# Encoder layer on one core: a fourth z unit, tile-wise waits and re-ordered block sums in the gate section; a one-operation T1, later evictions and later T4 lows in gate/up

## The chip, the cores and the metric

The kernel runs on one core of a Trainium2 chip. The metric is the device time in microseconds (us) of one execution; a kernel's time is the median of its runs. Five engines work from queues of their own, each strictly in its program's order, and meet only through semaphores: TensorE (PE, matrix products into PSUM banks), VectorE (DVE), ScalarE (ACT), GpSimd (POOL) and SyncE (SP), which here issues the DMAs.

## The reference, cut to what matters

One layer of a hybrid encoder on 1024 tokens and 16 meta tokens with 1024 columns, all in float32:

```
h    = rmsnorm(x);  proj = h @ w_in     # q|k|v|z|beta,a|B|C|x|gate_a|gate_b
o_dn = bidirectional gated DeltaNet(q, k, v, beta, a), normed, times silu(z)
y_a  = o_dn @ w_branch_dn
y_b  = (B * conv3(C * x)) @ w_branch_sc
x    = x + (sigmoid(gate_a) * y_a + sigmoid(gate_b) * y_b) @ w_out
gu   = rmsnorm(x) @ w_gate_up
x    = x + (silu(gu[:, :2816]) * gu[:, 2816:]) @ w_down
out  = rmsnorm(x) * final_norm_w
```

## The kernel before, in words

Every float32 operand is split into a high and a low part (`split`: ACT casts the high part, DVE subtracts to get the low one), and a product is three matmuls: high by high, high by low, low by high. So each operand of PE costs one ACT and one DVE operation before PE can read its second half.

**Phase 1** (to 946 us) runs the DeltaNet heads. Its order is written by a planner in the code (`pick`, `run_streams`, `pump`) under a manual schedule: the dense products of `w_in` (a *unit* is 128 columns: 8 blocks of k by 3 matmuls for each half of the tokens) fill PE between the steps of the scans. `ZH` of the eight z units are among these fillers; in the kernel before, five.

**The gate section** (946 to about 1089 us) computes the other z units (`z_rows`) and five gate pairs (`pair`, for columns `j` = 3 to 7 of `gate_a` and `gate_b`). A pair is computed in Strassen's way with seven block products instead of eight: the four blocks B11, B12, B21, B22 of the activations (2 halves of k by 2 halves of the tokens) give the sums T1 to T4 once (`moving_sums`, a generator whose steps the code interleaves with the z units), and the weights give S1 to S4 for each pair (`sums`, `stationary2`). The seven products, 12 matmuls each (`product`), are A11·B11, A12·B21, S2·T2, S1·T1, S3·T3, S4·B22 and A22·T4. They add up in two PSUM banks, `bank` and `bank2`, which are read ("evicted") between products: a partial sum that is read must be read before the next product adds to the same bank.

The z units, the sums and the first pair stand inside `border0`, a manual schedule for DVE, PE and ACT, so on these engines they keep the order in which the code writes them; a scheduler may put later work between them, and orders the rest. All tiles of this section come from the pool `tp`, which takes over the memory of phase 1's pools. Weights pass through four `raw` slots, loaded by SP.

**Branch, merge and output products** follow (to 1344 us), then **gate/up** (`part1` for A11·B11 and A12·B21, and the loop over `j` for the other five products, again with T1 to T4, for 22 column units), whose first units lie under a manual DVE schedule (`border`). There the moving blocks are built 128 tokens at a time by `norm_T` and `second_half`: T1 = B12 - B11, T2 = B22 - T1, T3 = B22 - B12, and T4 = B21 - T2 in `form_T4`. At the end stands the down product.

Of the kernel before, what the change touches and what calls it, by code (L numbers as in the profile page):

```python
# [16 lines left out]
P = 128  # L17
D = 1024
KT = 8
# [6 lines left out]
NC = 8  # L26
FF = 2816
NF = FF // P
ZH = 5
GH = 3  # L30
EPS = 1e-6
NEG = -1e30
# [16 lines left out]
def encoder_layer(ctx: ExitStack, tc: tile.TileContext, x, meta, norm1_w, w_in, w_ba,  # L49
# [128 lines left out]
    def sub(out, a, b):  # L178
        nc.vector.tensor_tensor(out=out, in0=a, in1=b, op=ALU.subtract)
# [6 lines left out]
    def norm_T(t, diag, hn, bank=psany):  # L186

        c = slice(t % 4 * P, t % 4 * P + P)
        pts = []
        for g in range(2):  # L190
            pt = bank().rearrange("p (k t) -> p k t", k=4)
            pts.append(pt)
            for k in range(4):
                kk = 4 * g + k
                piece = hn[:, kk * P:(kk + 1) * P]
                if diag is None:
                    transpose(pt[:, k], piece)
                else:
                    mm(pt[:, k], piece, diag, start=True, stop=True)
            if t < 4:  # L200
                split(*(m[:, :, c] for m in mov[("B11", "B21")[g]]), pt)
        if t < 4:
            return

        def blocks():
            second_half(c, pts)
        return blocks

    def second_half(c, pts):
        b11h, b11l = (m[:, :, c].bitcast(F32) for m in mov["B11"])  # L210
# [1202 lines left out]

    def sums(rg, ru, s2, s4_, s3, s1):
        g0, g1, u0, u1 = rg[:, 0:4], rg[:, 4:8], ru[:, 0:4], ru[:, 4:8]
        nc.vector.tensor_tensor(out=s1, in0=u0, in1=u1, op=ALU.add)
        sub(s3, g0, u0)
        sub(s2, s1, g0)
        sub(s4_, g1, s2)

    def stationary2(j, ru, sa, sb, A_):

# [8 lines left out]
        split(uh, ul, ru[:, 4:8])  # L1431
        A_["A22"] = uh, ul

    def product(po, a, b, add_to=False):

        (ah, al), (bh, bl) = a, mov[b]
        for k in range(4):
            bhk, blk = (m[k] if isinstance(m, list) else m[:, k] for m in (bh, bl))
            for x, y, i in ((ah, bhk, 0), (ah, blk, 1), (al, bhk, 2)):
                mm(po, x[:, k], y, start=k + i == 0 and not add_to, stop=k == 3 and i == 2, skip_group_check=add_to)  # L1440

    def moving_sums():

# [52 lines left out]
    def z_rows(h):  # L1496

        sz = s4(SEQ)
        for sl in (left, right):
            po = psany()  # L1500
            dense(po, z_units[h - ZH], hx, C0 + META + sl.start, 512)
            nc.scalar.activation(sz[:, sl], po, AF.Tanh, scale=0.5)
            yield
            nc.vector.scalar_tensor_tensor(out=sz[:, sl], in0=sz[:, sl], scalar=1.0, in1=po, op0=ALU.add, op1=ALU.mult)
        nc.sync.dma_start(z_d[h], sz)
        yield
# [3 lines left out]
    def pair_weights(n, j):  # L1510

        s_hl[n % 2] = big(("mB", "mA")[n % 2], [P, 2, 2, KT, P])
        if n == 0:
            u = big("w2", [P, 2, 4, P])
            u_hl[0] = u[:, 0], u[:, 1]
        elif n == 1:
            u_hl[1] = [tp.tile([P, 4, P], F32R, tag="t2", name=uid("u_hl"), bufs=2) for _ in range(2)]
        gh, gl = wtiles([P, KT, P])
        rg, ru = (rawtile([P, KT, P]) for _ in range(2))
        nc.sync.dma_start(rg, w_in[unit(OGA + j * P)])  # L1520
        nc.sync.dma_start(ru, w_in[unit(OGB + j * P)])
# [10 lines left out]
        return A_, first, second  # L1532

    def pair(n, j, A_, first, second):

        last = j == KT - 1
        o1, o2 = s4(), s4()
        bank = pss()
        if not last:
            if n:  # L1540
                first()
            product(bank, A_["A11"], "B11")
            nc.scalar.copy(o1[:, left], bank)  # L1543
            po = psz()
            product(po, A_["A12"], "B21")
            add(o1[:, left], po, o1[:, left])
            half_turn(o1[:, left])
        if last:
            first()
        if n:  # L1550
            second()
        bank2 = psz()
        if not last:
            product(bank, A_["S2"], "T2", True)
            nc.scalar.copy(o1[:, right], bank)
            product(bank2, A_["S1"], "T1")
            nc.scalar.copy(o2[:, right], bank2)
            product(bank, A_["S3"], "T3", True)
            add(o2[:, right], bank, o2[:, right])
            half_turn(o2[:, right])  # L1560
            product(bank2, A_["S4"], "B22", True)
            add(o1[:, right], bank2, o1[:, right])
            half_turn(o1[:, right])
            product(bank, A_["A22"], "T4", True)
            nc.scalar.activation(o2[:, left], bank, AF.Tanh, scale=0.5)
        else:
# [19 lines left out]
            half_turn(o1[:, right])  # L1586
        nc.sync.dma_start(ta_d[j], o1)
        nc.sync.dma_start(tb_d[j], o2)
        return o1
# [8 lines left out]
    z_units.append(wload(w_in, unit(OZ + (H - 1) * P)))  # L1598
    next(sums_of_blocks)
    next(z0)  # L1600
    next(z1)
    pair0 = pair_weights(0, GH)
    next(z1)
    pair0[1]()
    next(z1)
    pair0[2]()
    next(z2)
    next(sums_of_blocks)
    next(z2)
    next(sums_of_blocks)  # L1610
    next(sums_of_blocks)
    next(z2)
    next(sums_of_blocks)
    for n, j in enumerate(range(GH, KT)):
        o1 = pair(n, j, *(pair_weights(n, j) if n else pair0))
        if n == 0:
            border0.close()
# [115 lines left out]
    def part1(w, p1, sg):  # L1733
# [7 lines left out]
        add(sg, po, p1)  # L1741
        nc.scalar.activation(sg, sg, AF.Silu)
        return rg, ru, A_, p1, sg, bank

    def down_sums(k):

# [47 lines left out]
    for i in range(2):  # L1794
        split(t1s[i], t1s[2 + i], m32[1][:, 2 * i:2 * i + 2])
    p1_2 = [tp.tile([P, 512], F32, tag="t2", name=uid("t2"), bufs=2) for _ in range(2)]
    ahead.append(part1(w2, *p1_2))
    split(*mov["T3"], m32[3])
    u_hl[0] = big("w2", [P, 2, 4, P])
    for j in range(NF):  # L1800
        if j == 1:
            s_hl[1] = ap_.tile([P, 2, 2, KT, P], F32R, tag="al0", name="s_hl1")
            u_hl[1] = ap_.tile([P, 2, 4, P], F32R, tag="al2", name="u_hl1")
        rg, ru, A_, p1, sg, bank = ahead.pop(0) if ahead else part1(stationary1(j), sm[:, j % 2], sm[:, 2 + j % 2])
        if j:
            block22(j, ru, A_)
            sums(rg, ru, rg[:, 0:4], rg[:, 4:8], ru[:, 0:4], ru[:, 4:8])
# [25 lines left out]
        product(bank, A_["A22"], "T4", True)  # L1833
        mul(sg, bank, sg)
        if j == 0:
            border.close()
# [151 lines left out]
```

## Time and profile before

| | before |
|---|---|
| runs | 2009.29, 2007.11, 2007.06 us; median 2007.11 |
| the profiled execution | 2003.46 us, of it the span 2001.7 us |
| granted TensorE clock | 0.996 |
| PE busy | 1974.2 us (99%), 11999 matmuls |
| DVE / ACT / POOL busy | 1398.8 / 837.2 / 108.0 us |
| DMA | 251.00 MB, mean 125 GB/s |

PE is busy for 99% of the span, and the chain that ended last runs through it. A busy PE in this profile is not PE at its peak: a matmul's record lasts 0.39 us, while the next one starts 0.227 us after it, and records overlap. So lost time on PE is read from the starts of matmuls, not from its busy share: it hides in the short stretches where starts are further apart, or where the granted clock is low.

### The profile page before, as it was taken

The page shows a single profiled execution, that of the slowest core. Times are in us where ns is not written, and L with a number is a line of the kernel's source. Part 1 is how long each engine was busy: PE and PEld are TensorE (multiplying, and loading weights), DVE is VectorE, ACT ScalarE, POOL GpSimd, SP SyncE. Part 2 cuts the span into 40 slices and gives each one's busy share as a digit, 9 for nine tenths or more (in the row PEclk, how much of TensorE's full clock was granted, in tenths as well). Part 3 has the DMA queues.
Part 4 walks back from the last instruction along what each step waited for, and adds up shares of the span by engine and source line. Part 5 has one row for each costly group of instructions (what it writes and reads, how often), then busy time and mean ns, then how long its engine had stood idle before and what let it go on. Part 6 is the DMA issues. An engine that isn't in the chain of part 4 may idle for free.

```text
span 2001.7 us, 31862 instructions
## 1 busy us (share of the span) xinstructions
PE 1974.2 (99%) x11999; PEld 1720.7 (86%) x11999; DVE 1398.8 (70%) x3020; ACT 837.2 (42%) x1964; POOL 108.0 (5%) x407
## 2 busy tenths in 40 slices
PE   9999999999999999999899999999999999999998
PEld 8999999999999999888688888887888888888887
DVE  6888688888888888844945544469866666656575
ACT  6472354636464646343344221224323333334344
POOL 2011101010101010100000000000000000000000
PEclk9999999999999999999999999999999999999999
DMA  3122221212222212222236743123666345477654
GB/s 133 65 90 74 59 86 59 75 59 75 59 75 59 86 59 65 75 85 91 94 112 239 248 151 112 63 85 107 240 231 216 140 150 188 157 276 244 193 170 172
DMA packets 124689, 251.00 MB, mean 125 GB/s; under 512 B 44981, under 2 KB 46438, under 8 KB 122103
## 3 DMA queue, kind: packets, MB, share of 16 engines
q1 hardware_dynamic: 123959, 247.92, 37.2%
q8 instruction: 94, 1.54, 0.3%
q10 hardware_dynamic: 576, 1.05, 0.1%
q14 instruction: 60, 0.49, 0.1%
HBM read 180.67 MB, written 68.25 MB: 124 GB/s over the span
## 4 chain that ended last, share of the span: by engine, by line
PE 47%; DVE 3%; ACT 1%; issue 1%; DMA 1%; SPq 0%; DVEq 0%; ACTq 0%
PE pd L1440 13%; PE pe L1440 6%; PE pm L1440 4%; PE pe L1894 1%; PE pe L1895 1%; PE pe L1896 1%; PE pd L1894 1%; PE pd L1895 1%; PE pd L1896 1%; PE pd L135 1%; PE pd L134 1%; PE pe L135 1%; PE pe L134 1%; PE pd L136 1%; PE pe L136 1%; PE pm L1895 1%
## 5 line engine op out<-in xcount | busy, mean ns | idle before, releaser
L341 PE MATMUL pm<-hTh,wh 128*128 128x320 f32 (+4 forms) x1264 | 434.2, 349 | 0.4 <-ACT hTh L1103 0.2
L341 PE MATMUL pm<-al,wh 128*128 128x320 f32 (+4 forms) x1264 | 433.6, 348 | 0.0
L341 PE MATMUL pm<-hTh,wl 128*128 128x320 f32 (+4 forms) x1264 | 431.7, 347 | 0.0
L341 PEld LDWEIGHTS pm<-hTh,wh 128*128 128x128 f32 x1264 | 236.7, 188 | 12.6 <-issue 1.3
L341 PEld LDWEIGHTS pm<-hTh,wl 128*128 128x128 f32 x1264 | 237.0, 188 | 10.9 <-issue 0.4
L341 PEld LDWEIGHTS pm<-al,wh 128*128 128x128 f32 x1264 | 236.9, 188 | 10.3
L102 DVE TENSOR_TENSOR al<-raw,ring_h 128x1024 fp32r<-128x1024 f32 x73 | 88.6, 1223 | 64.8 <-ACT ring_h L101 64.4
L101 ACT CAST ring_h<-raw 128x1024 fp32r<-128x1024 f32 x73 | 76.8, 1053 | 107.1 <-PE pe L1896 35.5
L363 DVE SCALAR_TENSOR_TENSOR kq<-ra,wc,kq 128x520 f32<-128x520 f32 x128 | 96.6, 755 | 4.9 <-ACT kq L393 4.0
L990 DVE TENSOR_TENSOR wl<-raw,wh 128x512 fp32r<-128x512 f32 x114 | 77.4, 689 | 31.1 <-ACT wh L993 30.6
L889 ACT ACTIVATE w<-pd,small 128x128 f32<-128x128 f32 x128 | 39.8, 363 | 125.0 <-PE pd L882 124.3
L101 ACT CAST wh<-raw 128x1024 fp32r<-128x1024 f32 x48 | 50.4, 1050 | 77.7 <-PE pd L135 18.7
L500 DVE TENSOR_TENSOR fP<-fP,tm 128x135 f32<-128x135 f32 (+23 forms) x248 | 71.7, 289 | 5.1
L496 DVE TENSOR_TENSOR tm<-fP,fN 128x135 f32<-128x135 f32 (+23 forms) x248 | 71.5, 288 | 4.4
L993 ACT CAST wh<-raw 128x512 fp32r<-128x512 f32 x114 | 67.4, 621 | 3.7 <-issue 3.6
L102 DVE TENSOR_TENSOR wl<-raw,wh 128x1024 fp32r<-128x1024 f32 x48 | 58.5, 1220 | 13.6 <-ACT wh L101 13.4
L1409 DVE TENSOR_TENSOR b<-pd,b 128x512 f32<-128x512 f32 x22 | 15.2, 690 | 66.2 <-PE pd L1440 66.2
L1831 ACT ACTIVATE b<-b 128x512 f32<-128x512 f32 x22 | 13.9, 632 | 113.3 <-DVE b L1409 113.3
L1440 PE MATMUL pd<-b_hl,wh 128*128 128x512 f32 x176 | 54.4, 390 | 0.0
L856 ACT ACTIVATE jk<-NP 128x128 f32<-128x128 f32 x64 | 19.9, 311 | 78.8 <-DVE NP L852 77.7
L1440 PE MATMUL pd<-b,mB 128*128 128x512 f32 x204 | 50.7, 398 | 1.1 <-ACT s L1543 1.1
L876 DVE SCALAR_TENSOR_TENSOR r<-pd,negEG,vS 128x128 f32<-128x128 f32 x120 | 36.7, 345 | 20.9 <-PE pd L866 20.5
(590 smaller groups left out, 4724.6 us busy)
## 6 DMA issues: line engine op xcount, KB each, us to landing
raw<-in_w_in_dram SPq DMA_DIRECT2D x72, 512.0 KB
raw<-in_w_gate_up_dram SPq DMA_DIRECT2D x44, 512.0 KB
sums<-in_w_down_dram SPq DMA_DIRECT2D x22, 512.0 KB
t_d<-sums SPq DMA_DIRECT2D x11, 1024.0 KB
raw<-s_d SPq DMA_DIRECT2D x44, 256.0 KB
raw<-t_d SPq DMA_DIRECT2D x44, 256.0 KB
act_d<-b SPq DMA_DIRECT2D x43, 256.0 KB
raw<-act_d SPq DMA_DIRECT2D x33, 256.0 KB
```

Of the source, the lines that this page charges most:

```text
L101: nc.scalar.copy(hi, src)
L102: nc.vector.tensor_tensor(out=lo, in0=src, in1=hi.bitcast(F32), op=ALU.subtract)
L134: mm(po[:m, :n], wh[:, k, :m], xhk[:, t0:t0 + n], start=(k == 0), stop=False)
L135: mm(po[:m, :n], wh[:, k, :m], xlk[:, t0:t0 + n], start=False, stop=False)
L341: mm(po[:, :n], ww[:, k], f(k)[:, t0:t0 + n], start=i == 0, stop=i == 3 * KT - 1)
L363: nc.vector.scalar_tensor_tensor(out=acc, in0=raw[:, h0 + t:h0 + t + hn], scalar=wc[:, t, col:col + 1], in1=acc, op0=ALU.mult, op1=ALU.add)
L496: nc.vector.tensor_tensor(out=tv, in0=fP[:, 0:r, j:j + 1].broadcast_to([P, r, n]), in1=fN[:, j:j + 1, j + 1:32].broadcast_to([P, r, n]), o ...
L500: nc.vector.tensor_tensor(out=fP[:, 0:r, j + 1:32], in0=fP[:, 0:r, j + 1:32], in1=tv, op=ALU.subtract)
L990: nc.vector.tensor_tensor(out=u[1][1][:, k], in0=u[2][:, k], in1=u[1][0][:, k].bitcast(F32), op=ALU.subtract)
L993: nc.scalar.copy(u[1][0][:, k], u[2][:, k])
L1440: mm(po, x[:, k], y, start=k + i == 0 and not add_to, stop=k == 3 and i == 2, skip_group_check=add_to)
L1895: mm(bank[t], h_[:, c], l_[:, hi], start=False, stop=False)
```

## The change

`ZH` becomes 4: one z unit moves from phase 1's fillers into the gate section, which now has four (`z0` to `z3`). The pool `tp` is made with `reuse_waits="tile"`. The steps of the sums T1 to T4, the weights' sums of the first pair and now also those of the second pair (`block_sums`, split off `second`) are placed anew between the z units, and `pair` becomes a generator, so that the second pair's sums can stand inside the first pair. In every pair but the last S4·B22 moves ahead of S3·T3, and z units take their banks from `psz` (tags `m` and `e`). In gate/up, ACT copies B11 into the place of T1 while the first 512 tokens are turned, so that T1 is one subtraction instead of two; the evictions of `part1` for the second and third unit (an add on DVE and a SiLU on ACT each) move behind T4's split; and in the first unit's A22·T4 the four matmuls with T4's low part come last.

```
-ZH = 5
+ZH = 4
...
                 split(*(m[:, :, c] for m in mov[("B11", "B21")[g]]), pt)
+                if g == 0:
+                    nc.scalar.copy(m32[1][:, :, c], pt)
...
-        sub(t1, pts[0], b11h)
-        sub(t1, t1, b11l)
+        sub(t1, pts[0], t1)
...
-    tp = ctx.enter_context(tc.tile_pool(name="tp", bufs=1))
+    tp = ctx.enter_context(tc.tile_pool(name="tp", bufs=1, reuse_waits="tile"))
...
-    def product(po, a, b, add_to=False):
+    def product(po, a, b, add_to=False, lows_last=False):
+        terms = [(k, *t) for k in range(4) for t in ((ah, bh), (ah, bl), (al, bh))]
+        if lows_last:
+            terms.sort(key=lambda t: t[2] is bl)
...
-            po = psany()
+            po = psz()
             dense(po, z_units[h - ZH], hx, C0 + META + sl.start, 512)
...
         def second():
+            stationary2(n, ru, rg, ru, A_)
+
+        def block_sums():
             split(*u_hl[n % 2], ru[:, 4:8])
             A_["A22"] = u_hl[n % 2]
             sums(rg, ru, rg[:, 0:4], rg[:, 4:8], ru[:, 0:4], ru[:, 4:8])
-            stationary2(n, ru, rg, ru, A_)
...
+            product(bank, A_["S2"], "T2", True)
+            nc.scalar.copy(o1[:, right], bank)
+            product(bank2, A_["S1"], "T1")
+            nc.scalar.copy(o2[:, right], bank2)
+            yield
+            product(bank2, A_["S4"], "B22", True)
+            add(o1[:, right], bank2, o1[:, right])
+            half_turn(o1[:, right])
+            product(bank, A_["S3"], "T3", True)
+            add(o2[:, right], bank, o2[:, right])
+            half_turn(o2[:, right])
+            yield
+            product(bank, A_["A22"], "T4", True)
+            nc.scalar.activation(o2[:, left], bank, AF.Tanh, scale=0.5)
...
-    z0, z1, z2 = (z_rows(h) for h in range(ZH, H))
+    z0, z1, z2, z3 = (z_rows(h) for h in range(ZH, H))
...
+    next(z2)
+    weights0 = pair_weights(0, GH)
+    next(z2)
+    weights0[1]()
     next(sums_of_blocks)
     next(z2)
+    next(z3)
+    weights0[2]()
+    weights0[3]()
     next(sums_of_blocks)
+    next(z3)
     next(sums_of_blocks)
+    next(z3)
+    pair0 = pair(0, GH, *weights0)
+    weights1 = pair_weights(1, GH + 1)
+    next(pair0)
+    weights1[1]()
+    weights1[2]()
+    for _ in pair0:
+        pass
...
-    ahead.append(part1(w1, sm[:, 1], sm[:, 3]))
+    ahead.append(part1(w1, sm[:, 1], sm[:, 3], False))
...
-    ahead.append(part1(w2, *p1_2))
+    ahead.append(part1(w2, *p1_2, False))
+    late_evictions = [p[-1] for p in ahead[1:]]
...
             split(*mov["T4"], m32[2])
+            for f in late_evictions:
+                f()
...
-        product(bank, A_["A22"], "T4", True)
+        product(bank, A_["A22"], "T4", True, lows_last=j == 0)
```

At three places the order of the instructions moves. The names in the rows are tiles (with buffer numbers): `rb` holds phase 1's z rows, `mA` and `b` T1 to T4 and their sums, `s` outputs of the section, `raw` weights as loaded, `mB` and `mA` also S1 to S4, `wh`, `wl` and `w` high and low weights, `pd`, `pe`, `pm` PSUM banks.

DVE where the section begins, before, with the semaphores that a row waits for: the last weight split and z row of phase 1, then the first three sums.

```order
L102 TENSOR_TENSOR wl_12208<-raw_12209,wh_12207 128x1024 [waits DMAHW1_49,PE_49,Activation_49]
L478 SCALAR_TENSOR_TENSOR rb_12188<-rb_12188,pm_12161 128x512 [waits DMAHW0_49,Activation_49]
L179 TENSOR_TENSOR mA_12243<-hTh 128x2048 [waits DMAHW4_49,DMAHW3_49,DMAHW5_49,DMAHW0_49,DMAHW6_49,DVE_49,Pool_49]
L179 TENSOR_TENSOR b_2083_12244<-al_124 128x2048
L1409 TENSOR_TENSOR mA_12243<-mA_12243,b_2083_12244 128x2048 [waits DVE_49]
```

The same place now:

```order
L102 TENSOR_TENSOR wl_12142<-raw_12143,wh_12141 128x1024 [waits DMAHW6_49,PE_49,Activation_49]
L478 SCALAR_TENSOR_TENSOR rb_12122<-rb_12122,pm_12072 128x512 [waits DMAHW5_49,Activation_49]
L179 TENSOR_TENSOR mA_12177<-hTh 128x2048
L179 TENSOR_TENSOR b_2076_12178<-al_124 128x2048
L1409 TENSOR_TENSOR mA_12177<-mA_12177,b_2076_12178 128x2048 [waits DVE_49]
```

The first sum waited for five DMA queues, and waits for none now.

ACT ahead of S2·T2 of the first pair, before: the high parts of T3 and T4, a z unit's tanh, and the eviction of A11·B11 (L1543).

```order
L1457 CAST b_2081_12242<-b_2083_12244 128x2048 [waits DVE_49]
L1502 ACTIVATE s_2097_12366<-pd_12399 128x512
L1457 CAST b_2100_12427<-mA_12243 128x2048 [waits DVE_49,Activation_49]
L1543 COPY s_2101_12434<-pd_12436 128x512
L101 CAST mA_12536<-raw_12542 128x1024 [waits DVE_49]
```

And now, where that eviction is L1574:

```order
L101 CAST mB_12318<-raw_12322 128x1024 [waits DVE_49,Pool_49]
L101 CAST mB_12318<-raw_12323 128x1024
L1460 CAST b_2098_12396<-mA_12177 128x2048 [waits DVE_49,Activation_49]
L1505 ACTIVATE s_2096_12359<-pe_12401 128x512 [waits PE_49]
L1574 COPY s_2107_12439<-pd_12441 128x512 [waits DMAHW1_49,PE_49]
```

The eviction of A11·B11 stands behind T4's high part in both; T3's high part has moved far ahead of it, and the casts of S1 to S4 (`mB`) now stand next to it.

PE in the first pair, before: A11·B11 and A12·B21 of the first pair, A11·B11 of the second and two matmuls of the third pair, and then S2·T2, S1·T1, S3·T3 (`pd_12436` is `bank`, `pe_12465` `bank2`).

```order
L1440 MATMUL pm_12450<-hTh,wl_12320 128x512
L1440 MATMUL pd_12547<-hTh,wh_12539 128x512
L1440 MATMUL pd_12547<-al_124,wh_12539 128x512
...
L1440 MATMUL pd_12667<-hTh,wh_12659 128x512
L1440 MATMUL pd_12667<-al_124,wh_12659 128x512
L1440 MATMUL pd_12436<-b_2080_12241,mB_12317 128x512 x12
L1440 MATMUL pe_12465<-b_2079_12240,mB_12317 128x512 x12
L1440 MATMUL pd_12436<-b_2081_12242,mB_12317 128x512 x12
```

And now (`pd_12441` is `bank`, `pm_12478` `bank2`; `hTh,mB` and `al,mB` are S4·B22):

```order
L1443 MATMUL pe_12455<-hTh,wl_12321 128x512
L1443 MATMUL pd_12441<-b_2073_12175,mB_12318 128x512 x12
L1443 MATMUL pm_12478<-b_2072_12174,mB_12318 128x512 x12
L1443 MATMUL pm_12478<-hTh,mB_12318 128x512 x2
...
L1443 MATMUL pd_12441<-b_2074_12176,mB_12318 128x512 x12
L1443 MATMUL pd_12441<-b_2098_12396,w_2090_12319 128x512 x12
```

The 14 matmuls of later pairs no longer stand ahead of S2·T2, and two products in a row now go to the same bank, twice: S1·T1 and S4·B22, then S3·T3 and A22·T4.

More of the change, by code (lines that the diff above doesn't have):

```diff
@@ L1415, in sums @@
         g0, g1, u0, u1 = rg[:, 0:4], rg[:, 4:8], ru[:, 0:4], ru[:, 4:8]
[L1416 to L1419, printed above, removed]
+        tt = nc.vector.tensor_tensor
+        tt(out=s1, in0=u0, in1=u1, op=ALU.add)
+        tt(out=s3, in0=g0, in1=u0, op=ALU.subtract)
+        tt(out=s2, in0=s1, in1=g0, op=ALU.subtract)
+        tt(out=s4_, in0=g1, in1=s2, op=ALU.subtract)
     def stationary2(j, ru, sa, sb, A_):
@@ L1432, in block22 @@
         A_["A22"] = uh, ul
-    def product(po, a, b, add_to=False):
+    def product(po, a, b, add_to=False, lows_last=False):
         (ah, al), (bh, bl) = a, mov[b]
[L1437 to L1440, printed above, removed]
+        at = lambda m, k: m[k] if isinstance(m, list) else m[:, k]
+        terms = [(k, *t) for k in range(4) for t in ((ah, bh), (ah, bl), (al, bh))]
+        if lows_last:
+            terms.sort(key=lambda t: t[2] is bl)
+        for i, (k, x, y) in enumerate(terms):
+            mm(po, x[:, k], at(y, k), start=i == 0 and not add_to, stop=i == 11, skip_group_check=add_to)
     def moving_sums():
@@ L1530, in second, with pair @@
             sums(rg, ru, rg[:, 0:4], rg[:, 4:8], ru[:, 0:4], ru[:, 4:8])
-            stationary2(n, ru, rg, ru, A_)
-        return A_, first, second
-    def pair(n, j, A_, first, second):
+        return A_, first, block_sums, second
+    def pair(n, j, A_, first, block_sums, second):
         last = j == KT - 1
-        o1, o2 = s4(), s4()
+        o1, o2 = outs[n] = s4(), s4()
         bank = pss()
[L1539 to L1547, printed above, removed]
         if last:
             first()
-        if n:
+            block_sums()
             second()
[L1552 to L1563, printed above, removed]
-            product(bank, A_["A22"], "T4", True)
-            nc.scalar.activation(o2[:, left], bank, AF.Tanh, scale=0.5)
-        else:
+            bank2 = psz()
             product(bank, A_["S2"], "T2")
@@ L1586, in pair @@
             half_turn(o1[:, right])
+        else:
+            if n > 1:
+                first()
+                block_sums()
+            product(bank, A_["A11"], "B11")
+            nc.scalar.copy(o1[:, left], bank)
+            po = psz()
+            product(po, A_["A12"], "B21")
+            add(o1[:, left], po, o1[:, left])
+            half_turn(o1[:, left])
+            yield
+            if n:
+                second()
+            bank2 = psz()
+            product(bank, A_["S2"], "T2", True)
[9 more added lines that the diff above has]
+            half_turn(o2[:, right])
+            yield
+            product(bank, A_["A22"], "T4", True)
+            nc.scalar.activation(o2[:, left], bank, AF.Tanh, scale=0.5)
         nc.sync.dma_start(ta_d[j], o1)
         nc.sync.dma_start(tb_d[j], o2)
-        return o1
+        yield
+    outs = {}
     sums_of_blocks = moving_sums()
-    z0, z1, z2 = (z_rows(h) for h in range(ZH, H))
+    z0, z1, z2, z3 = (z_rows(h) for h in range(ZH, H))
     z_units.append(wload(w_in, unit(OZ + (ZH + 1) * P)))
@@ L1740, in part1 @@
         product(po, A_["A12"], "B21")
-        add(sg, po, p1)
-        nc.scalar.activation(sg, sg, AF.Silu)
-        return rg, ru, A_, p1, sg, bank
+        later = lambda: (add(sg, po, p1), nc.scalar.activation(sg, sg, AF.Silu))
+        if evict:
+            later()
+        return rg, ru, A_, p1, sg, bank, later
     def down_sums(k):
```

27 lines of the change are left out of this document (13 added, 14 removed).

## The prediction

> **What bounds the kernel now.** I read the first table of the page, then PE's list of waits, then PE's timeline where those waits lie, and there the starts of matmuls rather than their busy time.
>
> ```profile
> PE 1974.2 (99%) x11999; PEld 1720.7 (86%) x11999; DVE 1398.8 (70%) x3020; ACT 837.2 (42%) x1964; POOL 108.0 (5%) x407
> ...
> PE pd L1440 <- DVE s L1504: 7.7, 2, 5.9
> PE pd L1440 <- ACT b L101: 2.6, 1, 2.6
> ...
> PE pd L1440 <- ACT s L1543: 1.1, 1, 1.1
> ```
>
> PE bounds the kernel, so the change can only win what PE loses now, and the list of waits says that most of it lies on products (L1440) of the gate section and of the first gate/up unit. The windows show what these stretches cost (columns: stretch, length, busy time and instructions by engine, granted clock, DMA share, GB/s):
>
> ```profile
> 946.00:1015.50 69.50, 59.92 (x243) 47.60 (x242) 54.25 (x46) 25.13 (x30) 0.00 (x0) 0.93 0.26 89
> 985.30:991.40 6.10, 0.23 (x2) 0.05 (x1) 6.10 (x6) 1.77 (x2) 0.00 (x0) 0.85 0.12 50
> 991.40:996.50 5.10, 5.10 (x12) 3.75 (x12) 5.10 (x3) 1.67 (x2) 0.00 (x0) 0.51 0.00 0
> 996.50:1000.40 3.90, 0.95 (x3) 0.30 (x2) 3.90 (x6) 2.38 (x2) 0.00 (x0) 0.93 0.28 112
> 1000.40:1004.60 4.20, 4.17 (x12) 3.33 (x13) 4.20 (x4) 1.58 (x2) 0.00 (x0) 0.66 0.05 20
> 1385.20:1388.00 2.80, 0.19 (x2) 0.03 (x1) 2.73 (x5) 1.90 (x1) 0.00 (x0) 1.00 0.00 0
> 1388.00:1394.00 6.00, 5.37 (x15) 3.67 (x16) 5.18 (x5) 1.82 (x3) 0.00 (x0) 0.72 0.43 126
> ```
>
> PE stands at 985.3 to 991.4 while DVE is busy throughout, and then runs at a granted clock of 0.51 for 5.1 us and again of 0.66 for 4.2 us. Waits cost twice here: once standing, once in the clock. The rate at full clock:
>
> ```profile
> 945.96 0.39 PE L134 MATMUL pm<-hTh,wh 128*128 128x512 f32 x1
> 951.40 0.39 PE L134 MATMUL pe<-hTh,wh 128*128 128x512 f32 x1
> ...
> 1012.78 2.88 PE L1440 MATMUL pd<-b,w 128*128 128x512 f32 x12
> ```
>
> 24 matmuls take 951.40 - 945.96 = 5.44 us, 0.2267 each. From 945.96 to the end of the first pair's A22·T4 (1012.78 + 12 x 0.2267 = 1015.5) there are by the order 6 x 24 (z units) + 98 (products) = 242 matmuls, 54.9 us of work in 69.5. **The section loses 14.6 us**, about 4.3 of it to the clock (0.49 x 5.1 + 0.34 x 4.2 + some).
>
> Why DVE is late:
>
> ```profile
> 947.02 1.23 DVE L102 TENSOR_TENSOR wl<-raw,wh 128x1024 fp32r<-128x1024 f32 x1 [4.98 <-ACT wh L101]
> 948.17 0.68 DVE L478 SCALAR_TENSOR_TENSOR rb<-rb,pm 128x512 f32<-128x512 f32 x1
> 953.10 2.29 DVE L179 TENSOR_TENSOR mA<-hTh 128x2048 f32<-128x2048 f32 x1 [4.26 <-issue]
> 955.31 2.29 DVE L179 TENSOR_TENSOR b<-al 128x2048 f32<-128x2048 f32 x1
> 948.88 0.32 SPq L480 DMA_DIRECT2D z_d<-rb  x1
> ...
> 998.00 1.90 ACT L1457 CAST b<-mA 128x2048 fp32r<-128x2048 f32 x1 [4.93 <-DVE mA L1409]
> 999.81 0.58 ACT L1543 COPY s<-pd 128x512 f32<-128x512 f32 x1
> 1000.43 4.33 PE L1440 MATMUL pd<-b,mB 128*128 128x512 f32 x12 [1.14 <-ACT s L1543]
> ```
>
> The first sum starts at 953.10, 4.3 us after DVE came free: in the order it waits for five DMA queues, and the last store of a phase 1 z row went out at 948.88, so it waited for the old pools' last transfers. From then on DVE has almost no gap until T4. S2·T2 of the first pair starts at 1000.43, when ACT has evicted A11·B11 (999.81), which stands behind T4's high cast (998.00) in its queue.
>
> **The z unit and the wait by tile.** PE does the same matmuls; 48 of them move from phase 1's tail to the section. So phase 1 ends, and the section's time zero t0 lies, 48 x 0.2267 = 10.9 us earlier, at 935.1, and the section has 10.9 us more to cover the sums. Two covers have to hold:
>
> ```profile
> 933.07 0.28 DVE L936 TENSOR_SCALAR NP<-NP,small 128x128 f32<-128x128 f32 x1
> 935.08 0.60 PE L98 MATMUL pd<-ident,NP 128*128 128x128 f32 x4
> ...
> 953.04 0.33 SPq L119 DMA_DIRECT2D raw<-in_w_in_dram  x1
> 966.98 1.04 ACT L101 CAST wh<-raw 128x1024 fp32r<-128x1024 f32 x1
> ```
>
> The last four head transposes come 5 matmuls (1.1 us) earlier in PE's queue, at about 933.9; their input was ready at 933.35, and a weight split ahead of it on DVE is gone. I put that at nothing; if the cover were gone it would cost under 1 us. The weights of the third z unit went out on SP at 953.04 and were cast by 966.98, 13.9 us; now they go out about t0 + 3 and are cast at t0 + 16.7, which leaves as long. The fourth's follow at once and have 22 us.
>
> Without the DMA wait the first sum follows the z row split. In before that row started at 948.17, t0 + 2.2; one 512-column operation later is t0 + 2.8, where before it was t0 + 7.1. So 4.3 + 10.9 = 15.2 us are won for the sums, against the first pair's place on PE. They aren't all used. DVE's spacing by these rows is 2.21 us for 2048 columns (953.10 to 955.31), 1.15 for 1024 (947.02 to 948.17) and 0.60 for 512. By the order there stand, up to T4's last add, 10 + 11 + 11 of these, with 7 places where one feeds the next (0.1 each): 22.1 + 12.6 + 6.6 + 0.7 = 42 us. Following ACT's queue by its own rows I find 5.9 us of DVE waits for casts and tanhs that stand behind a high cast (1.9 us). T4's sum ends at t0 + 2.8 + 47.9 = 50.7. Then ACT: T4's high part 1.9, z3's tanh 0.5, the eviction of A11·B11 0.6: **S2·T2 can start at t0 + 53.8**. PE reaches it at t0 + 8 x 5.44 + 2 x 2.72 = 49.0, since no product of a later pair is put ahead of it now. Wait: 4.8 us. An error of 1 us in DVE's chain is 1 us here.
>
> After it the clock falls: the nearest row, after 5.9 us of standing, is 0.51 for 5.1 us, which loses 2.5; I take 2.4. [...]
>
> **The re-ordered pair.** In the first pair S4·B22 now follows S1·T1 in one bank, and A22·T4 follows S3·T3, with nothing between. What an eviction there costs:
>
> ```profile
> 1004.60 2.90 PE L1440 MATMUL pe<-b,mB 128*128 128x512 f32 x12
> 1007.34 2.88 PE L1440 MATMUL pd<-b,mB 128*128 128x512 f32 x12
> 1007.54 0.59 ACT L1557 COPY s<-pe 128x512 f32<-128x512 f32 x1 [1.21 <-PE pe L1440]
> 1010.32 0.69 DVE L1409 TENSOR_TENSOR s<-pd,s 128x512 f32<-128x512 f32 x1 [2.73 <-PE pd L1440]
> ```
>
> The product of 1004.60 is over at 1007.50, ACT's copy of its bank ends at 1008.13; the next matmul in that bank could start at 1008.2 instead of 1007.34: 0.85, and with the slower first matmuls 1.0. For DVE's add after S3·T3 likewise 1.0 (1010.32 + 0.69 against 1010.06). Below nothing it cannot be, since before a product of the other bank hid both. In the later pairs the scheduler puts 4 matmuls (0.91 us) between, which covers it: 0 to 0.1 each.
>
> The second pair's S1 to S4 come late: its `mA` casts stand on ACT behind the third pair's, whose A22 cast waits for the end of the first pair's A22·T4. From there: a cast 0.5, five 512-column operations on DVE 3.4, two lows and an add 2.9, a tanh, a cast and a low, 0.6 + 1.0 + 1.2 = 9.7, against 38 matmuls (8.6) on PE. Wait 1.1; with hops I take 1.5 (0 to 3).
>
> So the section loses 4.8 + 2.4 + 1.0 + 1.0 + 1.5 + 0.4 (restarts, hops) = 11.1 instead of 14.6: **-3.5 us** (-8 to +1).
>
> **Gate/up.**
>
> ```profile
> 1361.39 0.69 DVE L179 TENSOR_TENSOR al<-al,b_hl 128x512 f32<-128x512 f32 x1
> 1371.49 0.68 DVE L1409 TENSOR_TENSOR b<-pm,b 128x512 f32<-128x512 f32 x1
> 1375.29 0.68 DVE L1409 TENSOR_TENSOR t<-pe,t 128x512 f32<-128x512 f32 x1
> 1386.02 1.90 ACT L101 CAST b<-al 128x2048 fp32r<-128x2048 f32 x1 [5.47 <-DVE al L228]
> 1387.97 0.50 PE L1440 MATMUL pd<-b,w 128*128 128x512 f32 x1 [2.61 <-ACT b L101]
> 1391.36 1.22 DVE L102 TENSOR_TENSOR s_hl<-raw,s_hl 128x1024 fp32r<-128x1024 f32 x1
> 1393.90 2.44 PE L1440 MATMUL pm<-s,s_hl 128*128 128x512 f32 x10
> ```
>
> T1's second subtraction (1361.39, and its like a block later) goes; of 0.7 each some 1.0 remains behind ACT's casts. The evictions at 1371.49 and 1375.29 go from ahead of T4's cast: 1.1. So T4's high part starts at about 1384.0, not 1386.02, and A22·T4 at 1385.95, not 1387.97; its low four are ready in time (low part done 1388.2, PE there 1388.25). But the two evictions now stand ahead of the next unit's S1 low part: it starts at 1390.6 instead of 1391.36, and S1·T1's other 10 matmuls at 1391.9 (1393.90 before), after a wait of 2.7. Next late is S2's low part. I take **-1.6** (-3 to 0; a clock drop after that wait, 0.28 x 6, eats it). The copies of B11, four of 0.6 on an ACT that is busy 42%, cost nothing on the path.
>
> **Sum.** -3.5 - 1.6 = -5.1 us. The profiled execution took 2003.46, its span 2001.7: 1998.4, span 1996.6. The runs' median lies 3.65 above the profiled execution, so the same difference gives 2002.0. About 0.2% (4 us) is what a measurement here can tell from no change.
>
> **Rivals.**
> - *The clock stays up* in the 4.8 us wait. For it: the wait is shorter than the 5.9 that dropped it. Against it: 2.77 did. +2.4: -7.5, 1999.6. [...] Chance 0.15.
> - *More clock drops*: the waits of 1.0, 1.0 and 1.5 each follow within some us, as 1.85 and 1.14 did ahead of 1000.40, which cost 0.34 x 4.2 = 1.4. Two such: -2.2, 2004.9. Chance 0.2.
> - *The wait by tile does nothing*: the first sum still starts at t0 + 7.1. Then S2·T2 waits 9.1 and -0.8 is left, 2006.3. Against it: the order shows no wait there. Chance 0.06.
> - *Slower*: the same-bank evictions of the second to fourth pair. 6 places with a cover of 0.91 us; if at each the eviction stands behind one 1024-column cast (1.0), the wait is about 0.9, 5.4 in all, and three clock drops of 1.4 make 9.6: +4.5, 2011.6. It decides from 0.85 a place without drops. Against it: the scheduler put the cover there. Chance 0.09.
>
> My forecast has 0.5. Of it 0.42 is a gain over 4 us, with the first rival 0.57 for faster; the rest of it, the second, the third and 0.01 of the fourth make 0.35 for the same, 0.08 slower. The range leaves out the fourth and the ends of the others: 1997.5 (clock up and gate/up at its best) to 2006.5.
>
> **What would show it.** Right: first sum at t0 + 2.8 with no gap ahead; a PE wait of 4 to 6 us ahead of S2·T2, released by ACT's L1574, then a clock near 0.5; about 1 us each ahead of S4·B22 and A22·T4 of the first pair; A22·T4 of gate/up's first unit 2 us earlier after the unit's start. Wrong: PE waiting in the scan's tail, evictions late in the later pairs, or S2·T2 on time.

## The result, and the profile after

| | before | changed kernel |
|---|---|---|
| runs beside each other | 2008.74 us median (2007.06 to 2009.36, 5 runs) | 2000.5 us median (1997.71 to 2001.08, 5 runs) |
| ratio | | **0.9958**, 95% interval 0.9945 to 0.9971 |
| profiled execution | 2003.46, span 2001.7 | 2001.08, span 1999.3 |
| granted clock | 0.996 | 0.998 |

The change makes the kernel 8 us (0.4%) faster; a second session gave 0.9963 (0.9948 to 0.9977). PE's list of waits in the changed kernel (columns: who waits for whom, us in all, times, longest):

```profile
PE pd L1443 <- ACT s L1574: 4.9, 1, 4.9
PE pd L1443 <- DVE b L1409: 2.8, 2, 1.8
PE pm L1443 <- DVE s_hl L102: 2.3, 1, 2.3
...
PE pd L1443 <- ACT b L1847: 0.9, 2, 0.7
PE pd L1443 <- DVE s L1409: 0.8, 1, 0.8
PE pm L1443 <- ACT s L1586: 0.7, 1, 0.7
...
PE pd L1443 <- ACT b L101: 0.5, 1, 0.5
```

The 7.7 us on DVE's z rows and the 2.6 us on T4's cast in gate/up are gone. In their place stand one wait of 4.9 for ACT's eviction of A11·B11 (L1574), 2.3 for the low part of the next unit's S1, and a new one of 1.8 for an eviction on DVE (L1409). PE's timeline through the first pair, and three windows (stretch, length, busy us and instructions of PE, PEld, DVE, ACT, POOL, then granted clock, DMA share, GB/s):

```profile
988.96 5.01 PE L1443 MATMUL pd<-b,mB 128*128 128x512 f32 x12 [4.87 <-ACT s L1574]
993.81 2.88 PE L1443 MATMUL pm<-b,mB 128*128 128x512 f32 x12
997.37 0.50 PE L1443 MATMUL pm<-hTh,mB 128*128 128x512 f32 x1 [0.68 <-ACT s L1586]
...
1000.23 2.88 PE L1443 MATMUL pd<-b,mB 128*128 128x512 f32 x12
1003.95 3.01 PE L1443 MATMUL pd<-b,w 128*128 128x512 f32 x12 [0.84 <-DVE s L1409]
```

```profile
934.95:1006.70 71.75, 65.37 (x277) 52.98 (x276) 55.20 (x47) 24.60 (x30) 0.00 (x0) 0.95 0.28 99
988.95:993.80 4.85, 4.84 (x12) 3.84 (x13) 3.22 (x4) 2.31 (x4) 0.00 (x0) 0.55 0.27 108
993.80:1006.70 12.90, 11.38 (x49) 8.79 (x48) 6.31 (x9) 3.06 (x5) 0.00 (x0) 1.00 0.10 41
```

One wait of more than 1 us is left instead of three (5.9, 1.9 and 1.1 before), with one stretch of low clock behind it: from the start of the product at 988.96 to the start of the next it takes 4.85 us, not 2.72 (12 x 0.2267).

What the stages take in every profiled execution of this study: phase 1 up to the first matmul of the first z row in the section; from there to gate/up's first product; gate/up to the down stage's first matmul; the rest of the span. In kernels with four z units 48 matmuls (10.9 us) stand in the second stage instead of the first.

| kernel | phase 1 | section to gate/up | gate/up | down | span |
|---|---|---|---|---|---|
| before | 945.96 | 410.13 | 439.29 | 206.32 | 2001.7 |
| before, second profile | 946.43 | 410.44 | 439.40 | 206.43 | 2002.7 |
| wait by tile alone | 946.53 | 408.42 | 440.27 | 206.48 | 2001.7 |
| gate/up edits alone | 946.72 | 410.43 | 439.66 | 206.29 | 2003.1 |
| section edits alone | 935.25 | 416.47 | 440.77 | 205.71 | 1998.2 |
| changed | 934.95 | 416.99 | 441.08 | 206.28 | 1999.3 |
| changed, second profile | 934.70 | 416.38 | 438.47 | 206.15 | 1995.7 |
| changed, eviction first | 934.91 | 410.55 | 438.81 | 206.33 | 1990.6 |
| changed, one load | 935.98 | 417.06 | 437.33 | 207.33 | 1997.7 |
| changed, three z units | 947.42 | 413.70 | 438.82 | 205.86 | 2005.8 |
| changed, S3 first | 934.75 | 413.56 | 439.54 | 206.25 | 1994.1 |
| eviction first, S3 first | 934.99 | 408.70 | 440.04 | 206.77 | 1990.5 |
| eviction first, later evictions | 935.99 | 410.54 | 441.81 | 206.06 | 1994.4 |
| all four | 936.34 | 408.70 | 439.02 | 206.84 | 1990.9 |

The section stage of the same code repeats within 0.7 us, gate/up of the same code differs by 2.6 (441.08 and 438.47), phase 1 with the same number of z units by up to 1.6. So a difference of 1 to 2 us between single traces counts only where a wait in them accounts for it.

### The profile page after: what moved, and what is told of

Read it like the earlier page. It is cut to its first block, busy times and chain, and to the rows that moved or that the text cites. A ratio compares the mean times of both kernels' runs of the same rounds, so it can differ in the third digit from the quotient of the medians.

```text
span 1999.3 us, 31850 instructions
## 1 busy us (share of the span) xinstructions
PE 1972.3 (99%) x11999; PEld 1718.4 (86%) x11999; DVE 1396.7 (70%) x3015; ACT 838.6 (42%) x1967; POOL 107.0 (5%) x407
## 4 chain that ended last, share of the span: by engine, by line
PE 84%; DVE 8%; DMA 4%; ACT 3%; issue 1%; SPq 0%; DVEq 0%; ACTq 0%
PE pm L341 31%; PE pd L1443 10%; PE pe L1443 4%; PE pm L1443 3%; DMA sums<-in_w_down_dram 2%; PE pd L903 1%; PE pd L882 1%; PE pd L866 1%; PE pd L869 1%; PE pe L1927 1%; PE pe L1925 1%; PE pe L1926 1%; PE pd L899 1%; PE pe L603 1%; PE pd L1927 1%
## 5 line engine op out<-in xcount | busy, mean ns | idle before, releaser
L341 PE MATMUL pm<-hTh,wh 128*128 128x320 f32 (+4 forms) x1248 | 428.0, 348 | 0.4 <-ACT hTh L1103 0.2
L341 PE MATMUL pm<-al,wh 128*128 128x320 f32 (+4 forms) x1248 | 427.3, 348 | 0.0
L341 PE MATMUL pm<-hTh,wl 128*128 128x320 f32 (+4 forms) x1248 | 425.6, 346 | 0.0
L1409 DVE TENSOR_TENSOR b<-pd,b 128x512 f32<-128x512 f32 x22 | 15.2, 690 | 64.4 <-PE pd L1443 64.4
L1443 PEld LDWEIGHTS pd<-b,mB 128*128 128x128 f32 x204 | 39.5, 195 | 15.5 <-ACT s L1574 5.3
```

Source lines behind the costliest of these rows:

```text
L341: mm(po[:, :n], ww[:, k], f(k)[:, t0:t0 + n], start=i == 0, stop=i == 3 * KT - 1)
L1443: mm(po, x[:, k], at(y, k), start=i == 0 and not add_to, stop=i == 11, skip_group_check=add_to)
```

## The experiments

Each kernel was timed beside the kernel before, whose median was 2006.36 (31 runs), 2006.57 (14) and 2008.20 (9) in the three sessions (the third on another chip); kernels of different sessions are compared by their ratios to it.

**Session 1: the parts alone.**

*The kernel before, once more.* No edit.

> The kernel before, unchanged, profiled once more. The change's runs lie 8.2 us under those of before (2008.74 to 2000.5), the two profiled executions only 2.4 apart (2003.46 and 2001.08). Theory A: the first profiled execution of before was one of its fast ones, and an ordinary one loses 3 to 6 us more at a place that the trace can show; then this profile takes 2006 to 2009 and its extra loss lies in the gate section (945 to 1015) or at the first gate/up units. Theory B: what differs lies spread over the whole program or outside it; then this profile again takes about 2003.5, or is longer by the same share in every stage. Ratio to before: 1.000 within 0.0015 in both.

2006.28 us, ratio 1.0002 (0.9993 to 1.0011), the profiled execution 2004.49. The time lies 1.0 above theory B's and 1.5 under the least of theory A's; the trace is B's: the waits are the same (5.9 and 1.1 us in the section, 2.6 in gate/up), and the 1.0 us between the two spans lies in small pieces, 0.5 of it in phase 1. Before's 31 runs lie between 2004.14 and 2009.42; the first median of 2008.74, of five runs, lies near their upper end. The gap of 8.2 between the medians comes again in session 2 (2006.57 and 1998.11, 8.5 apart). The 2.4 between the profiles was small by two chances: before's first profile (2003.46) lies under all of those 31 runs, and the changed kernel's (2001.08) is the slowest of its five. The second profiles are 2004.49 and 1997.49, 7.0 apart (section 4.9, phase 1 0.9, gate/up 0.9, down 0.3).

*The wait by tile alone*, on the kernel before:

```
- tp = ctx.enter_context(tc.tile_pool(name="tp", bufs=1))
+ tp = ctx.enter_context(tc.tile_pool(name="tp", bufs=1, reuse_waits="tile"))
```

> Before with the wait by tile alone. Theory: the first sum starts 2.8 us after phase 1's end instead of 7.1, the DVE chain moves 4.3 us ahead, and of the first pair's waits the 5.9 us one falls to about 1.6 and with it some of the clock loss: 4 to 6 us faster, 2003 to 2005. Rival: DVE is held by ACT's casts and the z rows anyway, the sums end as late as before, 0 to 1 us.

2003.28 us, 0.9984 (0.9975 to 0.9993). DVE's timeline of this kernel at the start of the section, whose first matmul starts at 946.53, and then the windows of its long wait, of the product behind it, and of S2·T2:

```profile
948.74 0.68 DVE L478 SCALAR_TENSOR_TENSOR rb<-rb,pm 128x512 f32<-128x512 f32 x1
949.34 2.28 DVE L179 TENSOR_TENSOR mA<-hTh 128x2048 f32<-128x2048 f32 x1
```

```profile
984.60:988.80 4.20, 0.17 (x1) 0.00 (x0) 4.20 (x5) 1.70 (x2) 0.00 (x0) 1.00 0.00 0
988.85:993.00 4.15, 4.15 (x12) 2.96 (x12) 4.15 (x2) 1.70 (x2) 0.00 (x0) 0.65 0.00 0
997.91:1003.19 5.28, 5.28 (x12) 4.12 (x13) 4.34 (x4) 1.58 (x2) 0.00 (x0) 0.50 0.04 14
```

The first sum follows the z row at once, 2.8 us into the section instead of 7.1, so the mechanism is the one forecast. Of the 4.3 us only 1.7 to 2.0 arrive in the section stage, and two steps lose the rest. DVE has a new wait of 1.2 for a weight cast on ACT (up to 970.06), so S2·T2 starts only 3.1 earlier in the section, and the long wait falls from 5.9 to 4.1, not to 1.6. And S2·T2 then takes 5.3 us at a clock of 0.50, where it took 4.2 at 0.66 before. In time 3 us, between theory and rival.

*The gate/up edits alone*, on the kernel before (T1 from the copy of B11, `late_evictions`, `lows_last`, as in the change):

> Before with the gate/up edits alone. Theory: A22.T4 of the first unit starts about 2 us earlier in its unit and unit 1 follows 1.4 us earlier, but units 3 to 10 lose it again where DVE's sums for the down stage wait for their weights and PE for the evictions behind them: 0 within 1.5 us. Rival: what units 3 to 10 lost in the trace of after was chance or comes from elsewhere, and the 1.4 to 1.6 us stay: 2007.

2005.85 us, 0.9997 (0.9988 to 1.0006): as the theory had it, no gain that shows.

*The section edits alone*: the change with those gate/up edits taken out.

> The change without its gate/up edits: T1 in two subtractions, evictions of units 1 and 2 where they were, lows not last. Theory: the section keeps its gain (in the traces PE stands 4.2 us better at the start of gate/up), S2.T2 still waits 4.9 us, and the ratio lies within 0.001 of that of the change (0.995 to 0.997). Rival: the gate/up edits carry half of the 8 us or more, and this kernel is only 0 to 4 us faster than before (0.998 to 1.000).

2000.95 us, 0.9975 (0.9966 to 0.9985), just above the theory's 0.997 and clear of the rival but for its edge. The section carries about 5 of the 8 us (3.0 to 6.8 by the interval); what the gate/up edits add lies between the 0.6 us of the run before and, by difference, 2.4 to 3.4 us (0.9963 or 0.9958 against 0.9975), each uncertain by about 2 us or more.

**Session 2: single waits of the changed kernel.**

*The changed kernel once more.* No edit.

> The changed kernel, unchanged, in the same session as its variants. Theory: its gain is the section's (5.0 us alone, 0.9975) and little from gate/up (0.6 us alone): 0.9970 to 0.9975, 2000 to 2001.5, and the first ratio of 0.9958 was at the fast end. Rival: the two parts help each other and 0.9958 comes again, 1998.

1998.11 us, 0.9963 (0.9948 to 0.9977): the time is the rival's, the ratio lies between 0.9958 and the theory's range. The interval holds both, so this doesn't decide whether the parts help each other.

*T4's high cast behind the eviction.* A step of its own for the cast, and the last z row and A11·B11 ahead of it:

```
-        high("T4", t1)
+        yield
+        high("T4", t1)
...
             nc.scalar.copy(o1[:, left], bank)
+            if n == 0:
+                yield
...
     next(z3)
-    next(sums_of_blocks)
     next(z3)
     pair0 = pair(0, GH, *weights0)
     weights1 = pair_weights(1, GH + 1)
     next(pair0)
+    next(sums_of_blocks)
+    next(pair0)
+    next(sums_of_blocks)
```

> The changed kernel with T4's high cast behind the eviction of A11.B11 on ACT (the last z row's tanh and that eviction no longer wait for T4's sum). Theory: the 4.9 us wait ahead of S2.T2 is the ACT queue's order alone, T4 itself is needed only 11 us later: PE runs on at phase 1's end + 49.0, the wait and the 2.0 us of clock loss go, the two same-bank waits of about 0.9 stay: 5.5 to 7 us faster than the changed kernel. Rival: a low part or T4's low comes late instead, ahead of S1.T1, S3.T3 or A22.T4, and takes back 3 us or more: 0 to 4 us faster.

1993.26 us, 0.9936 (0.9923 to 0.9949): 4.9 us under the changed kernel of the same session, between rival and theory. In the changed kernel, ACT's and DVE's timelines at that place read

```profile
983.60 2.35 DVE L1409 TENSOR_TENSOR mA<-mA,al 128x1024 f32<-128x1024 f32 x2
986.04 1.90 ACT L1460 CAST b<-mA 128x2048 fp32r<-128x2048 f32 x1 [3.81 <-DVE mA L1409]
987.84 0.59 ACT L1505 ACTIVATE s<-pe 128x512 f32<-128x512 f32 x1
988.33 0.58 ACT L1574 COPY s<-pd 128x512 f32<-128x512 f32 x1
```

and in this one, with PE's and the window of the whole stretch:

```profile
982.10 0.59 ACT L1506 ACTIVATE s<-pe 128x512 f32<-128x512 f32 x1
982.59 0.58 ACT L1575 COPY s<-pd 128x512 f32<-128x512 f32 x1
986.00 1.92 ACT L1460 CAST b<-mA 128x2048 fp32r<-128x2048 f32 x1 [2.83 <-DVE mA L1409]
...
990.27 0.59 ACT L1589 COPY s<-pm 128x512 f32<-128x512 f32 x1
```

```profile
986.61 2.88 PE L1443 MATMUL pm<-b,mB 128*128 128x512 f32 x12
990.92 0.50 PE L1443 MATMUL pm<-hTh,mB 128*128 128x512 f32 x1 [1.43 <-ACT s L1589]
...
997.44 3.06 PE L1443 MATMUL pd<-b,w 128*128 128x512 f32 x12 [0.78 <-DVE s L1409]
```

```profile
934.91:1000.30 65.39, 63.18 (x277) 51.66 (x276) 55.01 (x47) 24.43 (x30) 0.00 (x0) 1.00 0.30 109
```

T4's cast starts at the same time in both, but the eviction no longer stands behind it: it is done at 983.2 instead of 988.9, S2·T2 runs without a wait, and the clock stays at 1.00. The section stage is 5.8 us shorter than in the second profile of the changed kernel, in the range of the theory; the wait ahead of S4·B22 grows from 0.7 to 1.4, because the copy of S1·T1's bank now stands behind that cast and what is queued after it.

*One transfer for the down stage's sums* in gate/up:

```
-        nc.sync.dma_start(r[:, 0], w_down[k * P:k * P + P, :])
-        nc.sync.dma_start(r[:, 1], w_down[(HK + k) * P:(HK + k + 1) * P, :])
+        nc.sync.dma_start(r, w_down.rearrange("(a k p) d -> k p a d", a=2, p=P)[k])
```

> The changed kernel with the two weight loads of the down stage's sums in gate/up as one transfer. Theory: in unit 3 and after, DVE stands in these sums up to 4.6 us for the second load, the eviction behind them is late and PE waits (1.8, 0.7 and 0.2 us in the profile); with one transfer, issued where the first load was, the wait for it shrinks by 3 us and those PE waits go: 1.5 to 3 us faster than the changed kernel. Rival: the transfer of 1 MB takes as long as both did, DVE waits as before: within 0.8 us.

1998.14 us, 0.9960 (0.9947 to 0.9973), the time of the changed kernel: the rival's number, but not its reason. DVE's row of waits for these loads in the changed kernel, in its second profile, and in this kernel:

```profile
DVE sums L179 <- DMA sums<-in_w_down_dram: 16.8, 10, 4.6
```

```profile
DVE sums L179 <- DMA sums<-in_w_down_dram: 13.1, 9, 4.5
```

```profile
DVE sums L179 <- DMA sums<-in_w_down_dram: 4.3, 4, 1.4
```

The wait is cut as the theory said, PE has no wait of 0.2 us or more between 1410 and 1780 any more, and gate/up takes 437.33 us, the least of all, if in part because the clock stayed at 1.00 behind another wait, of 2.3 us, in this trace (last section). About 1 us of PE waits (0.9 in the second profile) is too little to show in the time. The down stage of this profile is the longest of all (207.33; 205.71 to 206.84 elsewhere), and why is open.

*Three z units* in the section, the rest of the change kept (`ZH = 5`; the fourth z row's steps left out of the order, T3 and T4 one z row earlier):

> The changed kernel with three z units in the section as before the change, everything else of the change kept. Theory: the DVE chain up to T4 loses only the 2.4 us of one z row, PE loses 10.9 us of cover: S2.T2 waits about 13.4 us instead of 4.9, 8 to 9 us slower than the changed kernel, some 2008 to 2009. Rival: the wait by tile and the new order of the sums carry the gain, the z unit little: within 2 us of the changed kernel.

2006.66 us, 1.0002 (0.9993 to 1.0011): 8.55 us slower than the changed kernel, and no faster than before.

```profile
PE pd L1443 <- ACT s L1574: 11.9, 1, 11.9
```

```profile
997.95:1003.00 5.05, 5.01 (x12) 3.98 (x13) 3.42 (x4) 2.48 (x4) 0.00 (x0) 0.53 0.26 104
```

PE's waits and the product behind the longest: the theory's 8 to 9 us are there. The section stage is 8.2 us longer than that of the changed kernel's second profile (413.70 against 416.38 - 10.88), 7.0 of it the wait (11.9, not the 13.4 expected) and 0.8 the clock. In this order of the sums the whole gain hangs on the fourth z unit: it gives PE 10.9 us of work ahead of S2·T2. The rival is out.

**Session 3: the pair's order, and a faster kernel.**

*S3·T3 ahead of S4·B22*, as before the change: the two products change places with their evictions.

> The changed kernel with S3.T3 ahead of S4.B22 in every pair but the last, as before the change. Theory: in the first pair the waits of 0.84 ahead of S4.B22 and 1.0 ahead of A22.T4 go, since a product of the other bank lies between each eviction and the next use of its bank: 1.5 to 2 us faster than the changed kernel (ratio to before 0.995). Rival: T3's low part or an add stands in the way in that order and the change's order is there for a reason: a wait of 1 us or more ahead of S3.T3, no gain or slower.

1996.38 us, 0.9942 (0.9928 to 0.9955). Both waits are gone from the trace and the section stage is 2.8 us shorter than in the second profile of the changed kernel: 2.1 in the first pair (the two waits and the slower first matmuls behind them, 0.84 and 1.0 from start to start in the changed kernel's first profile) and 0.7 in pieces of about 0.1 in pairs two to four, which are gone too. The ratio lies 0.0021 under 0.9963, the way of the theory and more than its 2 us; the intervals overlap.

*Both: eviction first and S3·T3 first.*

> T4's high cast behind the eviction of A11.B11, and S3.T3 ahead of S4.B22. Theory: the section then loses only its restarts, under 1 us: 2 to 2.5 us faster than with the first edit alone (1.59 and 0.95 us waited there), ratio to before 0.992 to 0.993. Rival: T4's low part or the add after S3.T3 now ends last ahead of A22.T4: within 1 us of the first edit alone.

1991.97 us, 0.9922 (0.9909 to 0.9934); the section stage is 1.85 us shorter than with the first edit alone. Not under 1 us of loss, though. PE's waits in it:

```profile
PE pd L1443 <- ACT s L1587: 1.0, 1, 1.0
...
PE pd L1443 <- DVE s L1409: 0.4, 1, 0.4
```

The copy of S2·T2's bank (L1587) stands on ACT behind T4's cast and the two weight casts after it, and S3·T3 waits 1.0 for it now. The 0.4 is the rival's add ahead of A22·T4.

*Eviction first, and the evictions of units 1 and 2 later still:*

```
             split(*mov["T4"], m32[2])
-            for f in late_evictions:
-                f()
...
         if j == 0:
+            for f in late_evictions:
+                f()
             border.close()
```

> T4's high cast behind the eviction of A11.B11, and in gate/up the evictions of units 1 and 2 after the last multiplication of unit 0 instead of after T4's low part, so behind the low part of unit 1's S1. Theory: S1.T1 of unit 1 starts 1.2 to 1.8 us earlier in its unit (it waits 2.3 us for that low part), S2.T2 then waits for its own low part, which comes no earlier: 0.5 to 1.2 us faster than with the first edit alone. Rival: the wait moves to S2.T2 whole: 0.

1993.00 us, 0.9927 (0.9914 to 0.9939): 0.0009 under the first edit alone, with intervals that overlap almost whole, so nothing that shows. The wait for S1's low part fell to 1.1 and one for S2 came in its place:

```profile
PE pd L1443 <- ACT s_hl L101: 2.1, 1, 2.1
...
PE pm L1443 <- DVE s_hl L102: 1.1, 1, 1.1
```

3.2 us together, where the first edit alone has 2.3 and 0.2: the rival, and 0.7 more.

*All four edits.*

> All four edits: T4's high cast behind the eviction, S3.T3 ahead of S4.B22, the late evictions later still, one transfer for the down stage's sums. Theory: they lie at different places and add: 2 to 4 us faster than with the first edit alone, ratio to before 0.991 to 0.993. Rival: DVE is the next bound in gate/up and gives the smaller ones back: within 1.5 us of the first edit alone (0.993 to 0.994).

1991.45 us, **0.9918** (0.9904 to 0.9931), the fastest kernel here: 17 us under before, some 9 under the changed kernel by the ratios. The ratio is the theory's, but that all four add is not shown: most of it is the first two edits (0.9922), and the other two add nothing that can be told apart.

## Why the prediction was right, step by step

- **Phase 1 and the head transposes.** Forecast 935.1 and no wait at 933.9; they were 934.95, and 933.83 without a wait.
- **The first sum.** Forecast 2.8 us into the section:

```profile
937.78 2.28 DVE L179 TENSOR_TENSOR mA<-hTh 128x2048 f32<-128x2048 f32 x1
```

937.78 - 934.95 = 2.83, and 2.81 in the kernel with the wait by tile alone. The rival in which that wait does nothing is out.

- **S2·T2.** T4's sum was to end at 50.7 and S2·T2 to start at 53.8 after a wait of 4.8. The sum ended at 985.95 (983.60 + 2.35), 51.0; the start was 988.96, 54.0; the wait 4.87. DVE's waits for casts and tanhs on the way sum to 5.5 us (forecast 5.9). Eviction first shows that it was ACT's order alone.
- **The clock.** Forecast a loss of 2.4; the product took 4.85 instead of 2.72, 2.1 lost at a granted clock of 0.55. The 2.77 us set against the rival in which the clock stays up are those ahead of A22·T4 in gate/up's first unit before (1385.20 to 1387.97), with 0.72 over the 6 us that follow. That rival is out here, and so is the one with more drops: the stretch behind it with the waits of 0.68 and 0.84 ran at 1.00.
- **The same-bank evictions.** Forecast 1.0 each; from start to start, less 2.72, they cost 0.84 (993.81 to 997.37) and 1.0 (1000.23 to 1003.95). The 4 matmuls between products covered them in the later pairs: no wait of 0.2 us there, some 0.1 at each place and 0.7 in all by the starts, which the sum had put at nothing. The slower rival is out.
- **The first pair as a whole.** From t0 to the end of its A22·T4 there are by the order 8 x 24 + 7 x 12 = 276 matmuls, 62.6 us of work, in 71.75 (the first window of the result): 9.2 us lost, where the terms up to there gave 9.6 (4.8 + 2.4 + 1.0 + 1.0 + 0.4) and before lost 14.6.
- **The second pair's S1 to S4** was the mis-sized term: 1.5 forecast, 0.3 measured. I counted to the end of the low part. Its rows on ACT, DVE and PE:

```profile
1014.62 1.98 ACT L101 CAST mA<-raw 128x1024 fp32r<-128x1024 f32 x2
1015.69 2.36 DVE L102 TENSOR_TENSOR mA<-raw,mA 128x1024 fp32r<-128x1024 f32 x2 [1.64 <-ACT mA L101]
1015.71 0.74 PE L1443 MATMUL pd<-b,mA 128*128 128x512 f32 x2
```

The first two matmuls use the high part alone, and start as the low part does; the low part's first use comes four matmuls of another product later. So the 1.2 us of the low part do not belong on the path. The section's gain was 4.0 us (416.99 - 10.88 = 406.11 against 410.13) to 4.9 (second profiles), not 3.5.

- **Gate/up** came out step by step, but not in sum. The stage starts 4.15 us earlier than before (1351.94 instead of 1356.09), so add 4.15 to compare. Rows of ACT, PE and DVE:

```profile
1379.73 1.91 ACT L101 CAST b<-al 128x2048 fp32r<-128x2048 f32 x1 [3.33 <-DVE al L228]
1381.70 2.11 PE L1443 MATMUL pd<-b,w 128*128 128x512 f32 x8 [0.48 <-ACT b L101]
...
1386.28 1.22 DVE L102 TENSOR_TENSOR s_hl<-raw,s_hl 128x1024 fp32r<-128x1024 f32 x1
1387.55 2.56 PE L1443 MATMUL pm<-s,s_hl 128*128 128x512 f32 x10 [2.34 <-DVE s_hl L102]
```

T4's cast 1383.88 (forecast 1384.0), A22·T4 1385.85 (1385.95), S1's low part 1390.43 (1390.6), S1·T1's ten matmuls 1391.70 (1391.9) after 2.34 (2.7). By the last product of unit 1 (1400.28 against 1405.87) it is 1.4 us ahead. But then come these, in the changed kernel:

```profile
1489.35 2.15 DVE L179 TENSOR_TENSOR sums<-sums 128x512 f32<-128x512 f32 x3 [4.63 <-DMA sums<-in_w_down_dram]
1491.41 0.68 DVE L1409 TENSOR_TENSOR b<-pd,b 128x512 f32<-128x512 f32 x1
1492.15 3.06 PE L1443 MATMUL pd<-b,w 128*128 128x512 f32 x12 [1.80 <-DVE b L1409]
```

DVE stands 4.6 us in the down stage's sums for weights, and the eviction that frees PE's bank is queued behind them. The whole stage took 1.8 us more than before in this profile and 0.9 less in the next; the -1.6 followed the path to unit 1 and not past it. The gate/up edits alone gain 0.6 us (1.8 either way), so the forecast for this part isn't borne out, though not excluded.

  All the traces together tell where it went. Up to unit 1's last product the stage takes 49.7 to 50.3 us in the four kernels without the gate/up edits, and 48.1 to 48.8 in seven of the eight that have them as the change does (49.7 in the other). Some 140 us into the stage, at the place of the rows above, PE then loses 0.7 to 2.0 us in all seven of these eight that keep the two loads, and nothing in the one with a single load. Without the edits that loss came in two kernels of four (1.4 and 1.6 us), so the edits aren't its only cause. The average over the stage is 439.5 us for the seven and 439.9 for the four: some 0.4 of the forecast 1.6 is left.

- **The sum.** -5.1 us was forecast, and 1998.4 for a profiled execution: the two came to 2001.08 and 1997.49. The median of 2000.5 lies 1.5 under 2002.0, and that it lies so near is in part luck. The forecast stands on before's median of three runs, 2007.11; with two more it was 2008.74, so an error of 3.1 in the gain (8.2 against 5.1) shows as 1.5 in the time. The forecast also took the 3.65 us between before's median and its profile over to the changed kernel. It is no constant: 1.8 in before's second profile, -0.6 and 0.6 in the changed kernel's. By ratio the gain is 8.4 and 7.4 us, more than the 5.1: 0.5 to 1.4 of it more in the section, the rest phase 1 and chance that these runs don't settle.

## What to carry to other kernels

An eviction that PE waits for belongs ahead, in its engine's queue, of any cast that waits for a long chain on another engine: here that one place was worth 5 us, more than any part of the change but the z unit. Cover for a serial chain comes from moving matmuls that need nothing of it in front of the first product that does; count how far the chain really ends behind, to the first operand used and not to the last. A gain at the head of a stage can be lost again further on, where a DMA wait on one engine holds up an eviction queued behind it (4.6 us on DVE and 1.8 on PE in the changed kernel); look for it in several traces, since the same code differed by 2.6 us there.

## What the runs showed of the hardware

In these traces the granted clock fell after a single wait as short as 1.9 us, but not each time: it was 0.62 over the product at 1487.40 behind 1.87 us in the kernel with the later evictions, and 1.00 over the one at 1492.15 behind 1.80 us in the changed kernel. The ten S1·T1 matmuls of gate/up's unit 1, behind the same wait of 2.3 us: second profile of the changed kernel, then the one with one load.

```profile
1386.60:1390.20 3.60, 3.52 (x10) 2.83 (x11) 3.60 (x7) 1.05 (x1) 0.00 (x0) 0.65 0.89 312
```

```profile
1388.60:1391.50 2.90, 2.57 (x10) 1.80 (x10) 2.90 (x5) 1.08 (x2) 0.00 (x0) 1.00 0.90 295
```

Of the eight traces with that wait the clock fell in four (0.59 to 0.66 over these matmuls) and stayed at 1.00 in four; over the product behind the waits of 4 to 12 us in the section it was 0.50 to 0.65 in the six traces where it was read (0.55, 0.65 and 0.53 in the rows above). So the price of a wait of 2.3 us here is 2.3 or some 3 us (the windows over the ten matmuls are 3.5 to 3.8 us long where it fell, 2.9 where it didn't), and no run shows what decides which; that of a wait of 4 us or more is the wait and some 2 us (1.4 with the wait by tile alone, 1.5 in the second profile of the changed kernel, 2.3 with three z units, 2.4 before).
